# Seven block products instead of eight in the input product of a recurrent layer

## The chip, the cores and the metric

The kernel runs on one core of a Trainium2 chip. The metric is the device time of one execution in microseconds; of several runs the median is given. The core has five engines that run side by side, each with its own queue of instructions that it works off in order: TensorE (PE: matmuls; the loading of its weights is shown as PEld), VectorE (DVE), ScalarE (ACT), GpSimd (POOL) and SyncE (SP, which here only issues transfers). Matmuls read SBUF and add into banks of PSUM; DVE and ACT read both, POOL reads SBUF alone. Engines wait for each other by semaphores.

## The reference

One step of a streaming encoder with two layers over 640 tokens: 512 of a prompt and 8 sample sequences of 16. The first layer is recurrent (an RG-LRU), the second is attention over a shared K and V. What matters here is the first layer, cut from the reference:

```python
hn = rms_norm(x, g_pre[l]) * (1.0 + scale) + shift
...
xb, zg = jnp.split(hn @ w_in, 2, axis=-1)          # (640, 2048) @ (2048, 8192)
xb, conv_new = causal_conv(xb, conv0, conv_w, conv_b)
y, hT = rg_lru(xb, h0, w_r, b_r, w_i, b_i, lam)    # two block-diagonal gate products inside
return (y * jax.nn.silu(zg)) @ w_out, hT, conv_new
```

`hn @ w_in` is the input product: all 640 tokens against 8192 columns, of which the first 4096 are the branch that goes through the convolution and the recurrence (the x branch) and the others the gate branch.

## The kernel before

Everything is float32 in and out. Each operand of a large product is split into a high and a low part in the type fp32r, and a product takes three matmuls (`mm3`, lines 90 to 94): high times high, high times low, low times high. For weights, `wsplit` (line 66) loads a raw tile by SP, ACT copies it to the high part `wh` (line 78), and DVE subtracts to get the low part `wl` (line 79).

The program has stages. In the **start** the squares of x give the norm, the adaLN weights of 33.5 MB stream in (`ada_first`, eight buffers) and give scale and shift for 128 features at a time (a K step; there are 16), and each finished step of the normed input is multiplied at once with five column tiles of 128 columns (`fill`). In the **recurrent part** 16 blocks of 256 features follow (`recurrent_block`, line 436). A block j has:

- two column tiles of the x branch, 2j and 2j+1: `proj_unit` runs 16 K tiles, two halves of 320 tokens each, three matmuls each, in two banks `psu` and `psv`; then ACT evicts to `hb`, ACT and DVE do the convolution (`ca`, `xf`), and the result is split (`xh`, `xl`);
- two column tiles of the gate branch: the same products, and the sigmoid times the value on ACT and DVE (`zs`);
- 48 matmuls of the two gates (`psg2`), ACT's sigmoids, and for each of the two halves of 128 features the RG-LRU: a tanh and a square root on ACT, on DVE a reciprocal of 640 columns, several products, the scan, and the product with `zs`; POOL keeps the states and issues the store to DRAM (`yd`).

The weights of the recurrent part come from the generator `plan` in the order of their use; `ahead` (line 428) keeps up to three pairs of split tiles (`WB`) of 1024 columns ready, four raw tiles behind them. After the recurrent part comes the output product (`out_product`), then K and V, then attention; these stages are not touched, except for the pools of SBUF that they use.

The Tile framework puts the instructions of each engine in an order of its own by their place in the program and its idea of their durations, and adds the semaphores. At run time each engine keeps that order.

## Time and profile before

| | |
|---|---|
| time, median of 3 runs | 2955.97 us (2954.01 to 2956.94) |
| profiled execution, span | 2950.4 us; its own time is not listed apart from the three |
| TensorE busy in the span | 2904.2 us, 98% |
| recurrent part, first matmul of `psu` to first of the output product | 145.65 to 1089.01 us |
| matmuls in it | 59 column tiles x 96, and 768 of the gates |
| granted TensorE clock in it | 1.00 |

A row of groups in the profile names the line, the engine, the operation, what it writes and reads, and how often; then total busy time and mean nanoseconds of one, then idle time ahead of them and what ended it. A row of stretches gives for a stretch the busy time of each engine with its count of instructions, then the granted clock, the DMA share and GB/s. A row of the timeline has its start, its duration, the engine, the line and the operation; neighbours of one kind are merged ("x3").

### The profile page before, as it was taken

To read this page: it belongs to the slowest core of one execution; us is meant where nothing else is said; L and a number is where in the kernel's file an instruction comes from. 1 tells how busy PE (TensorE), PEld (TensorE's weight loads), DVE (VectorE), ACT (ScalarE), POOL (GpSimd) and SP (SyncE) were. 2 spreads that over 40 slices of the span, in tenths; PEclk is the share of its full clock that TensorE was granted. 3 is DMA by queue.
4 is the path that set the end of the run, shared out by engine and by line. 5 is a ranking of instruction groups with operands and counts; after the bars stand their busy time and mean duration, and the time that the engine had idled before them with its cause. 6 is when DMAs were issued, how large, how long until landed. Compare 5 with 4: busy or idle time off the path is not lost.

```text
span 2950.4 us, 48268 instructions
## 1 busy us (share of the span) xinstructions
PE 2904.2 (98%) x19414; PEld 2604.3 (88%) x19414; DVE 1890.5 (64%) x2491; ACT 1460.6 (50%) x2227; POOL 297.1 (10%) x518
## 2 busy tenths in 40 slices
PE   6999999999999999999999999999999999999998
PEld 5899999999999997778877999877989998897787
DVE  5686655666655666734468877777667666677435
ACT  3364434444434455634357666674455555556323
POOL 0010000000000000001021422000100000001000
PEclk9999999999999999999999999999999999999999
DMA  9822222222222237645477666663655556555736
GB/s 346 293 100 86 86 83 85 82 95 86 82 87 82 82 121 232 195 123 183 139 263 241 214 212 215 207 218 95 199 172 180 177 177 199 177 182 182 221 103 226
DMA packets 224512, 481.43 MB, mean 163 GB/s; under 512 B 17416, under 2 KB 106632, under 8 KB 223136
## 3 DMA queue, kind: packets, MB, share of 16 engines
q1 hardware_dynamic: 215216, 441.99, 46.8%
q0 software_dynamic: 9072, 36.37, 3.5%
q8 instruction: 152, 2.49, 0.3%
q14 instruction: 72, 0.59, 0.1%
HBM read 441.17 MB, written 37.11 MB: 162 GB/s over the span
## 4 chain that ended last, share of the span: by engine, by line
PE 94%; DVE 2%; DMA 2%; ACT 1%; issue 1%; POOL 0%; SPq 0%; DVEq 0%; POOLq 0%; ACTq 0%
PE acc L92 7%; PE acc L93 7%; PE acc L94 7%; PE psh L92 5%; PE acck L92 5%; PE psh L94 5%; PE psh L93 5%; PE acck L93 5%; PE acck L94 5%; PE psu L92 5%; PE psv L92 5%; PE psv L93 5%; PE psu L93 5%; PE psu L94 5%; PE psv L94 5%; PE psa L187 2%
## 5 line engine op out<-in xcount | busy, mean ns | idle before, releaser
L79 DVE TENSOR_TENSOR wl<-wr,wh 128x1024 fp32r<-128x1024 f32 (+2 forms) x382 | 448.9, 1176 | 443.2 <-ACT wh L78 441.7
L78 ACT ACTIVATE wh<-wr 128x1024 fp32r<-128x1024 f32 (+2 forms) x382 | 383.0, 1009 | 572.1 <-PE acc L94 219.1
L93 PE MATMUL acc<-wl,yh 128*128 128x512 f32 x960 | 376.3, 393 | 5.5 <-DVE wl L79 5.3
L92 PE MATMUL acc<-wh,yh 128*128 128x512 f32 x960 | 376.9, 393 | 4.3 <-ACT wh L78 2.1
L94 PE MATMUL acc<-wh,yl 128*128 128x512 f32 x960 | 375.2, 392 | 0.3 <-DVE yl L547 0.3
L175 DVE TENSOR_TENSOR wa<-wa,wa 128x1024 f32<-128x1024 f32 (+1 forms) x256 | 310.0, 1246 | 25.7 <-ACT wa L174 23.7
L92 PE MATMUL psh<-nh,wh 128*128 128x320 f32 x1024 | 323.9, 316 | 0.0
L94 PE MATMUL psh<-nh,wl 128*128 128x320 f32 x1024 | 318.9, 311 | 0.0
L93 PE MATMUL psh<-nl,wh 128*128 128x320 f32 x1024 | 317.4, 310 | 0.0
L174 ACT ACTIVATE wa<-wa 128x1024 bf16<-128x1024 f32 x256 | 262.9, 1052 | 67.9 <-DVE wa L175 49.0
L92 PE MATMUL psu<-hh,wh 128*128 128x320 f32 x944 | 291.7, 309 | 0.0
L92 PE MATMUL psv<-hh,wh 128*128 128x320 f32 x944 | 291.7, 309 | 0.0
L93 PE MATMUL psv<-hl,wh 128*128 128x320 f32 x944 | 291.7, 309 | 0.0
L94 PE MATMUL psv<-hh,wl 128*128 128x320 f32 x944 | 291.7, 309 | 0.0
L94 PE MATMUL psu<-hh,wl 128*128 128x320 f32 x944 | 291.7, 309 | 0.0
L93 PE MATMUL psu<-hl,wh 128*128 128x320 f32 x944 | 291.7, 309 | 0.0
L92 PEld LDWEIGHTS acc<-wh,yh 128*128 128x128 f32 x960 | 180.8, 189 | 52.9 <-issue 8.7
L93 PEld LDWEIGHTS acc<-wl,yh 128*128 128x128 f32 x960 | 181.1, 189 | 45.2 <-DVE wl L79 8.5
L94 PEld LDWEIGHTS acc<-wh,yl 128*128 128x128 f32 x960 | 181.3, 189 | 38.7 <-DVE yl L547 1.3
L92 PEld LDWEIGHTS psh<-nh,wh 128*128 128x128 f32 x1024 | 192.3, 188 | 19.3 <-DVE ql L881 12.6
L94 PEld LDWEIGHTS psh<-nh,wl 128*128 128x128 f32 x1024 | 192.4, 188 | 0.5 <-DVE wl L79 0.2
L93 PEld LDWEIGHTS psh<-nl,wh 128*128 128x128 f32 x1024 | 192.4, 188 | 0.1
(275 smaller groups left out, 6093.1 us busy)
## 6 DMA issues: line engine op xcount, KB each, us to landing
wa<-w_ada_dram SPq DMA_DIRECT2D x192, 512.0 KB, 4.8
wr<-w_in_a_dram SPq DMA_DIRECT2D x118, 512.0 KB, 3.7
wr<-w_out_a_dram SPq DMA_DIRECT2D x96, 512.0 KB, 4.1
wr<-w_in_b_dram SPq DMA_DIRECT2D x64, 512.0 KB, 5.1
ck<-cache_k_dram SPq DMA_DIRECT2D x64, 512.0 KB, 6.5
cv<-cache_v_dram SPq DMA_DIRECT2D x64, 512.0 KB, 5.4
wr<-w_out_b_dram SPq DMA_DIRECT2D x56, 512.0 KB, 4.0
wr<-w_v_dram SPq DMA_DIRECT2D x40, 512.0 KB, 4.2
```

Of the source, the lines that this page charges most:

```text
L78: nc.scalar.activation(hi[:, :n], raw[:, :n], AF.Copy)
L79: nc.vector.tensor_tensor(lo[:, :n], raw[:, :n], hi[:, :n].bitcast(F32), ALU.subtract)
L92: mm(out, sh, mh, start=start, stop=False, **kw)
L93: mm(out, sh, ml, start=False, stop=False, **kw)
L94: mm(out, sl, mh, start=False, stop=stop, **kw)
L174: nc.scalar.activation(parts[i], raw, AF.Copy)
L175: nc.vector.tensor_tensor(parts[2] if i else raw, raw, parts[i], ALU.subtract)
L187: nc.tensor.matmul(ps[32 * j : 32 * j + 32, :], self.c3[:, 4 * g + j, :], ws[j // 2][i][:, j % 2, :], start=g + i == 0, stop=g == 3 and i ...
```

## The change

Twelve of the 16 K tiles of the input product are taken as six pairs, (0, 1), (2, 3) and so on. For a pair of K tiles, a pair of column tiles and the two halves of the tokens, the product is one of 2x2 by 2x2 blocks. It is now computed by seven block products instead of eight, in Winograd's form of Strassen's scheme, and the four other K tiles (`PLAIN`) as they were.

- In the start `combine` makes four sums of blocks of the normed input for each pair of K tiles (`S1` to `S4`), on POOL, and splits them on ACT and DVE. They stay in SBUF for all 30 pairs of column tiles. The start multiplies four column tiles instead of five, and w_ada has five buffers instead of eight.
- `pair_weights` yields nine split tiles for a pair of column tiles: seven of 768 columns (b11, and sums of blocks) and two of 512 for the plain K tiles. The four sums are made by POOL in place in the raw tiles: the second set is b12 - b11 in the tile of b11, the third b22 minus that in the same tile, the sixth b22 - b12 in the tile of b12, the seventh b21 minus the third in the tile of b11.
- `pair_product` runs the sets in this order with accumulators in four banks: X11 into a, S1 into c, S2 into a again, X12 and the plain K tiles into b, S3 into a again, X22 and plain into d, S4 and plain into c, plain into a. Between two uses of a bank ACT copies what it holds (`keep`); the last evictions are DVE additions of a bank and such a copy.
- Three products with 640 columns a half block go from DVE to POOL: with the gate branch's sigmoid, of the input gate with x, and of the result with the gate branch.
- `ahead` keeps four pairs of split tiles (768 columns) with seven raw tiles. The states are stored and the parameters loaded block by block. The pools of the later stages are opened after the recurrent part, over the memory that it used, with waits by tile.

The core of the diff:

```diff
+NP = 6
+PLAIN = range(2 * NP, KD)
+WQ = NP * P
+WV = len(PLAIN) * P
+X12, X22, X11, S1, S2, S3, S4 = range(7)
+EARLY = (0, 1, FT, FT + 1)
...
-            ws = self.adap.tile([P, 4, 256], F32, tag="wa", name="wa0", bufs=8)
+            ws = self.adap.tile([P, 4, 256], F32, tag="wa", name="wa0", bufs=5)
...
+    def combine(self, rp, slot, even, odd):
+        nc, G = self.nc, self.nc.gpsimd
+        a, b = slice(0, HALF), slice(HALF, T)
+        t = [rp.tile([P, HALF], F32, tag=f"s{i}", name=f"s{i}", bufs=1) for i in range(4)]
+        G.tensor_tensor(t[0], even[:, b], odd[:, b], ALU.add)
+        G.tensor_tensor(t[1], t[0], even[:, a], ALU.subtract)
+        G.tensor_tensor(t[2], even[:, a], even[:, b], ALU.subtract)
+        G.tensor_tensor(t[3], odd[:, a], t[1], ALU.subtract)
+        for i, v in zip((S2, S3, S4, S1), (t[1], t[2], t[3], t[0])):
+            c = slice(HALF * i, HALF * i + HALF)
+            nc.scalar.activation(slot[:, 0, c], v, AF.Copy)
+            nc.vector.tensor_tensor(slot[:, 1, c], v, slot[:, 0, c].bitcast(F32), ALU.subtract)
...
+    def pair_weights(self, q):
+        w, G = self.I["w_in_a"][q], self.nc.gpsimd
+        at = iter(range(0, 4 * WQ, WQ))
+        b11, b12, b22, b21 = (self.wload(w[:, o : o + WQ]) for o in at)
+        yield self.hilo(b11, P)
+        G.tensor_tensor(b11, b12, b11, ALU.subtract)
+        yield self.hilo(b11, P)
+        G.tensor_tensor(b11, b22, b11, ALU.subtract)
+        yield self.hilo(b11, P)
+        yield self.hilo(b21, P)
+        G.tensor_tensor(b12, b22, b12, ALU.subtract)
+        v = self.wload(w[:, 4 * WQ : 4 * WQ + WV])
+        yield self.hilo(v, P)
+        yield self.hilo(b12, P)
+        G.tensor_tensor(b11, b21, b11, ALU.subtract)
+        yield self.hilo(b11, P)
+        v = self.wload(w[:, 4 * WQ + WV :])
+        yield self.hilo(b22, P)
+        yield self.hilo(v, P)
...
+        def seven(ps, i, first):
+            hi, lo = self.weights()
+            c = slice(HALF * i, HALF * i + HALF)
+            for n, x in enumerate(self.pairs):
+                self.mm3(ps, hi[:, n, :], lo[:, n, :], x[:, 0, c], x[:, 1, c], first and n == 0, n == NP - 1, **kw)
+            self.ahead()
...
+        a, c = bank("pa7"), bank("pc7")
+        seven(a, X11, True)
+        p1 = keep(a)
+        seven(c, S1, True)
+        p5 = keep(c)
+        seven(a, S2, False)
+        u2 = keep(a)
+        b = bank("pb7")
+        seven(b, X12, True)
+        w = self.weights()
+        plain(b, w, 0)
+        evac(0, 0, b, p1)
+        d = bank("pd7")
+        plain_d = lambda: plain(d, w, 1)
+        seven(a, S3, False)
+        u3 = keep(a)
+        seven(d, X22, True)
+        plain_d()
+        self.ahead()
+        evac(0, 1, d, u3)
+        seven(c, S4, False)
+        w = self.weights()
+        plain(c, w, 0)
+        evac(1, 0, c, u2)
+        plain(a, w, 1)
+        self.ahead()
+        evac(1, 1, a, p5)
...
+            G.tensor_tensor(zs[h], zs[h], g, ALU.mult)
...
-            V.tensor_tensor(ig, ig, xf[h], ALU.mult)
+            G.tensor_tensor(ig, ig, xf[h], ALU.mult)
...
-            V.tensor_tensor(hh, hh, zs[h], ALU.mult)
-            nc.gpsimd.dma_start(self.yd[P * f : P * f + P, :], hh)
+            G.tensor_tensor(hh, hh, zs[h], ALU.mult)
+            G.dma_start(self.yd[P * f : P * f + P, :], hh)
+        G.dma_start(self.O["state"][:, 2 * j : 2 * j + 2, :], st)
...
+            self.WB, self.RB, self.WW = 4, 7, WQ
```

Where the instructions of a middle block stand on their engines shows in three places. The first is POOL around the end of a block's second RG-LRU half. Before (`g` is the state sequence, `st` the kept states, `hb` the convolution's input):

```order
L520 COPY st<-g_5743 128x1
L521 COPY st<-g_5743 128x8
L523 DMA yd<-g_5743 128x640
L448 MEMSET hb 128x3
L449 COPY hb<-pv 128x8x3
L456 COPY st<-hb 128x3
L457 COPY st<-hb 128x24
```

And now:

```order
L664 COPY st<-g_4861 128x8
L665 TENSOR_TENSOR g_4861<-g_4861,zs 128x640
L667 DMA out_state_dram<-st 128x72
L666 DMA yd<-g_4861 128x640
L451 TENSOR_TENSOR wr<-wr 128x768
L583 COPY st<-hb 128x3
L584 COPY st<-hb 128x24
L456 TENSOR_TENSOR wr<-wr 128x768
L453 TENSOR_TENSOR wr<-wr 128x768
L460 TENSOR_TENSOR wr<-wr 128x768
```

The four weight sums (lines 451 to 460) of the next pair, that of the gate branch, stand behind the product and the two stores of the RG-LRU half, and the sum for the sixth set (456) ahead of that for the third (453).

The second is ACT from there on, where the convolution's start (`ca`), the split of its result (`xh`) and the weights' high parts (`wh`) meet. Before:

```order
L461 ACTIVATE ca<-hb,pv 128x664
L78 ACTIVATE wh<-wr 128x1024
L470 ACTIVATE xh<-xf 128x640
L452 ACTIVATE hb<-psu 128x320
L78 ACTIVATE wh<-wr 128x1024
L452 ACTIVATE hb<-psv 128x192
L454 ACTIVATE hb<-psv 128x8x16
L461 ACTIVATE ca<-hb,pv 128x664
```

And now:

```order
L588 ACTIVATE ca<-hb,pv 128x664
L86 ACTIVATE wh<-wr 128x768 x3
L597 ACTIVATE xh<-xf 128x640
L588 ACTIVATE ca<-hb,pv 128x664
L86 ACTIVATE wh<-wr 128x512
L498 ACTIVATE keep<-pa_6491 128x320
L86 ACTIVATE wh<-wr 128x768
L498 ACTIVATE keep<-pc_6492 128x320
```

The evictions are gone from ACT, and the copy of bank a after the first block product (`keep<-pa`) stands behind five splits and convolution steps of the block.

The third is DVE at the same place: from the scan of the second half (line 519 before, 662 now) on. Before:

```order
L519 SCALAR_TENSOR_TENSOR g_3335<-q,g_3335 128x640
L464 SCALAR_TENSOR_TENSOR xf<-hb,pv,ca 128x512
L522 TENSOR_TENSOR g_3335<-g_3335,zs 128x640
L466 SCALAR_TENSOR_TENSOR xf<-hb,pv,ca 128x128
L79 TENSOR_TENSOR wl<-wr,wh 128x1024
L471 TENSOR_TENSOR xl<-xf,xh 128x640
```

And now:

```order
L662 SCALAR_TENSOR_TENSOR g_5505<-q,g_5505 128x640
L87 TENSOR_TENSOR wl<-wr,wh 128x768
L568 TENSOR_TENSOR hb<-pd_5690,keep 128x192
L568 TENSOR_TENSOR hb<-pd_5690,keep 128x8x16
L590 SCALAR_TENSOR_TENSOR ca<-hb,pv,ca 128x664
L87 TENSOR_TENSOR wl<-wr,wh 128x768
L590 SCALAR_TENSOR_TENSOR ca<-hb,pv,ca 128x664
L591 SCALAR_TENSOR_TENSOR xf<-hb,pv,ca 128x512
L568 TENSOR_TENSOR hb<-pc_5575,keep 128x320
L87 TENSOR_TENSOR wl<-wr,wh 128x768
L568 TENSOR_TENSOR hb<-pa_5574,keep 128x192
L568 TENSOR_TENSOR hb<-pa_5574,keep 128x8x16
```

Three low parts of 768 columns stand between the convolution steps where one of 1024 stood, and the evictions of the four accumulators are here now.

More of the change, by code (lines that the diff above doesn't have):

```diff
@@ L189, in ada @@
             yield
-        m = self.mp.tile([P, 512], F32, tag="mod", name="msb", bufs=2)
+        m = self.more.tile([P, 512], F32, tag="mod", name="msb", bufs=2)
         nc.scalar.activation(m, ps, AF.Copy)
@@ L301, in norm_rows @@
             else:
-                sq = self.mp.tile([P, T], F32, tag="mod", name="sq", bufs=2)
+                sq = rp.tile([P, T], F32, tag="row", name="sq", bufs=4)
                 nc.scalar.activation(sq, x, AF.Square)
@@ L314, in spread @@
         nc = self.nc
-        dg = self.mp.tile([P, T], F32, tag="mod", name="diag", bufs=2)
+        dg = rp.tile([P, T], F32, tag="row", name="diag", bufs=4)
         for t in range(TT):
@@ L402, in proj_part @@
                          **(dict(skip_group_check=True) if shared else {}))
-    def proj_unit(self, f, banks=None):
-        if f in self.begun:
-            return self.begun[f]
-        u, v = banks or (self.acc("psu"), self.acc("psv"))
-        unit = (f, [(u[:, :HALF], 0, HALF, False), (v[:, :HALF], HALF, T, False)])
-        for kc in range(2):
-            self.proj_part(unit, range(8 * kc, 8 * kc + 8), self.weights())
-        self.ahead()
-        return unit[1]
     def plan(self):
-        I = self.I
-        for kc in range(2):
-            yield I["w_in_a"][3, :, 8 * kc : 8 * kc + 8, :], P
+        yield from self.pair_weights(1)
@@ new lines, with conv_rows @@
+    HW = 3 + TP + NB * (TS + 3)
+    S0 = 3 + TP
+    def conv_rows(self, j, ep):
+        G = self.nc.gpsimd
+        pv = ep.tile([P, 2, 40], F32, tag="pv", name="pv", bufs=3)
+        self.nc.sync.dma_start(pv, self.I["lru"][:, 2 * j : 2 * j + 2, :])
+        rows = []
+        for h in range(2):
+            hb = ep.tile([P, self.HW + 1], F32, tag="hb", name="hb", bufs=2)
+            G.memset(hb[:, 0:3], 0.0)
+            G.tensor_copy(hb[:, self.S0 : self.HW].rearrange("p (b t) -> p b t", t=TS + 3)[:, :, 0:3], pv[:, h, 8:32].rearrange("p (b t) -> p b t", t=3))
+            rows.append(hb)
+        return pv, rows
@@ L1109, in heads @@
         return out
-    WB = 3
+    ABUFS = {"A": NP, "V": KD - 2 * NP}
     AB = (3, 4)
```

287 lines of the change are left out of this document (174 added, 113 removed).

## The prediction

> **What bounds the kernel now.** I read the busy shares and the chain of waits first, then the stretches of the first layer's recurrent part, then the groups of DVE, ACT and POOL in it.
>
> ```profile
> span 2950.4 us, 48268 instructions
> PE 2904.2 (98%) x19414; PEld 2604.3 (88%) x19414; DVE 1890.5 (64%) x2491; ACT 1460.6 (50%) x2227; POOL 297.1 (10%) x518
> ...
> PE 94%; DVE 2%; DMA 2%; ACT 1%; issue 1%; POOL 0%; SPq 0%; DVEq 0%; POOLq 0%; ACTq 0%
> ...
> 145.65:208.90 63.25, 63.25 (x434) 63.25 (x433) 54.88 (x72) 40.76 (x63) 6.55 (x19) 1.00 0.26 88
> 208.90:1060.00 851.10, 851.10 (x5805) 851.10 (x5805) 526.72 (x623) 367.43 (x536) 69.94 (x192) 1.00 0.26 87
> ```
>
> TensorE is the bound. In the stretch that the change rewrites (the last two rows; columns PE, PEld, DVE, ACT, POOL, granted clock, DMA share, GB/s) it has no gap at all, at full clock, and its pace is 851.10/5805 = 0.1466 us a matmul. The 0.31 us of a single record overlaps with its neighbours, so matmuls are priced by the pace. DVE has 62% there, POOL 8%. The span lies 5.6 us under the median of 2955.97; I make the sum in the span and add that.
>
> **What it saves on TensorE.** A pair of 128-column tiles cost 2 x 16 x 2 x 3 = 192 matmuls of 320 columns. Now the twelve paired K tiles cost 7 x 6 x 3 = 126 and the four plain ones 48, so 174. Thirty pairs lie outside the start; column tile 2, which was in the start, comes back (96). A middle block (two pairs and 48 gate matmuls) goes from 432 to 396 matmuls, at the pace from 63.3 to 58.1 us; there are 14 of them. The two blocks ahead go from 384 to 444, from 56.3 to 65.1. If TensorE stays full, this sums to 14 x -5.28 + 8.8 = -65 us. That is the most the change can bring, and it asks the other engines for more in less time.
>
> **What it adds.** The splits of the weights go from 10 a block (eight of 1024, two of 512 columns) to 20 (fourteen of 768, six of 512), since seven sums of blocks have more elements than four blocks. And where a tile of weights lasted 48 matmuls (7 us) with three tiles ahead, one now lasts 18 (2.6 us) with four ahead: the lead falls from some 20 us to 8 to 10. The loads are not what comes late: a pair still brings 2.1 MB, DMA is at 26% there, and seven raw tiles let the next pair's loads start during the pair ahead.
>
> ```profile
> L79 DVE TENSOR_TENSOR wl<-wr,wh 128x768 fp32r<-128x768 f32 x8 | 7.6, 949 | 1.1 <-ACT wh L78 1.1
> ...
> L507 DVE RECIPROCAL q<-q 128x640 f32<-128x640 f32 x28 | 116.2, 4150 | 0.5
> L463 DVE SCALAR_TENSOR_TENSOR ca<-hb,pv,ca 128x664 f32<-128x664 f32 x52 | 47.2, 907 | 3.1 <-ACT ca L461 2.4
> L519 DVE TENSOR_TENSOR_SCAN g<-q,g 128x640 f32<-128x640 f32 x27 | 40.2, 1488 | 0.5
> L511 DVE TENSOR_TENSOR g<-g,g 128x640 f32<-128x640 f32 x27 | 22.4, 829 | 0.4
> L79 DVE TENSOR_TENSOR wl<-wr,wh 128x512 fp32r<-128x512 f32 x26 | 18.0, 693 | 77.3 <-ACT wh L78 76.9
> L506 DVE TENSOR_SCALAR q<-g 128x640 f32<-128x640 f32 x27 | 13.3, 494 | 9.1 <-ACT g L504 7.6
> L482 DVE TENSOR_TENSOR zs<-zs,psu 128x320 f32<-128x320 f32 x26 | 12.7, 488 | 139.9 <-ACT zs L481 139.9
> ...
> L466 DVE SCALAR_TENSOR_TENSOR xf<-hb,pv,ca 128x128 f32<-128x128 f32 x26 | 9.0, 347 | 0.0
> ```
>
> POOL gets eight weight sums of 768 columns and six products of 640 a block, where it had only short copies. Their prices come from its two-operand work elsewhere: 0.51 us for 128 columns and 1.30 for 512, so 2.06 ns a column, 1.83 us for 768 and 1.57 for 640.
>
> ```profile
> 2109.40 0.51 POOL L924 TENSOR_TENSOR e<-e,mask 128x128 f32<-128x128 f32 x1 [0.36 <-ACT e L908]
> 1363.93 1.30 POOL L646 TENSOR_TENSOR oacc<-oacc,gm 128x512 f32<-128x512 f32 x1 [72.86 <-ACT jk L590]
> L523 POOL DMA_DIRECT2D yd<-g x32 | 17.7, 552 | 36.0 <-DVE g L522 19.8 <-DVE xf L466 16.2
> L521 POOL COPY st<-g 128x8 f32<-128x8 f32 x32 | 6.1, 191 | 0.0
> ```
>
> A block asks 8 x 1.83 + 6 x 1.57 = 24 us of POOL. That would be no matter if POOL and DVE ran side by side, but the trace says that they do not:
>
> ```profile
> 1615.31 10.06 POOL L735 TENSOR_TENSOR wr<-wr,vec 128x1024 f32<-128x1024 f32 x4 [11.16 <-issue]
> 1618.46 7.99 DVE L738 TENSOR_TENSOR wl<-wr,wh 128x1024 fp32r<-128x1024 f32 x3 [0.59 <-ACT wh L737]
> ...
> 1640.39 4.76 DVE L175 TENSOR_TENSOR wa<-wa,wa 128x1024 f32<-128x1024 f32 x4
> ...
> 1362.40 2.05 DVE L644 TENSOR_TENSOR oacc<-acc,oacc 128x512 f32<-128x512 f32 x3 [0.23 <-PE acc L94]
> ```
>
> While POOL worked, three DVE splits took 7.99 us, 2.66 each; with POOL idle four subtractions of that size took 4.76, 1.19 each. They take turns, one whole instruction each. The last row has one operand in PSUM; it ran beside the POOL product at 1363.93 without growing (0.68 each). So DVE work on two SBUF tensors adds to POOL's and does not overlap it.
>
> **The loop that sets a block.** With the matmuls cheaper and the lead short, what decides is whether weights come in time. I follow one block from the end E of the gate-branch products, every step behind the one that it waits for or that stands ahead of it in its engine's order. In a full queue neighbours overlap by 0.05 us (four of 1.22 in 4.76), which I take off.
>
> ```profile
> L78 ACT ACTIVATE wh<-wr 128x768 fp32r<-128x768 f32 x8 | 6.7, 836 | 0.7 <-DMA wr<-w_in_a_dram 0.7
> ...
> L498 ACT ACTIVATE g<-psg,pv 128x320 f32<-128x320 f32 x108 | 51.7, 528 | 1.1
> L508 ACT ACT_TABLE_LOAD x28 | 35.9, 1283 | 0.5
> L461 ACT ACTIVATE ca<-hb,pv 128x664 f32<-128x664 f32 x26 | 24.5, 944 | 2.3
> L504 ACT ACTIVATE g<-g,k 128x640 f32<-128x640 f32 x27 | 22.6, 837 | 0.4
> L470 ACT ACTIVATE xh<-xf 128x640 fp32r<-128x640 f32 x26 | 19.3, 741 | 54.7 <-DVE xf L466 54.7
> L78 ACT ACTIVATE wh<-wr 128x512 fp32r<-128x512 f32 x26 | 16.3, 628 | 78.6 <-PE psv L93 78.6
> L452 ACT ACTIVATE hb<-psu 128x320 f32<-128x320 f32 x27 | 11.9, 439 | 99.8 <-PE psu L94 99.8
> ```
>
> 1. ACT: one split (0.84), the gate branch's sigmoid (as the tanh, 0.84), two gate sigmoids (1.06), tanh (0.84): E+3.6.
> 2. DVE from the first half's TENSOR_SCALAR to the second half's scan: two RG-LRU halves of 8.64 (reciprocal 4.15, scan 1.49, two products 1.64, two TENSOR_SCALAR 0.98, small ones 0.38), five splits of 768, two of 512, one eviction: 23.9, less 25 overlaps, 22.7: E+26.3.
> 3. POOL takes its turns in that stretch: a product, a sum and two copies fall outside the reciprocals, which I let run beside POOL: 3.6: E+29.9.
> 4. Behind the scan: DVE's next split (0.95), then POOL's two copies, the product with the gate branch, and two DMA issues, 3.0, all ahead of the next pair's first weight sum in POOL's order: E+33.9.
> 5. First sum 1.83; ACT's high part 0.84; POOL is by then in the sum for the sixth product, which holds DVE's low part back to E+37.9; low part 0.95; one convolution step 0.91 that DVE has next; third sum 1.83: E+41.6. Each sum works in place on the tile that the split before it reads, so they can't run ahead of each other.
> 6. ACT's high part of the third set 0.84, DVE's low part 0.95, then the two evictions of the last accumulator (0.33 each, 320 columns being 0.49) and the convolution's last step (0.35), which ACT needs for its split of x (0.74), the second half's convolution start (0.94), a split (0.63), and only then its copy of the first product (0.44): E+47.1, less a dozen overlaps, E+46.5.
> 7. That copy is what the third product waits for, since it adds into the same bank. From there 138 matmuls remain to the next E: 20.2 us.
>
> So a block takes 66.7 us, 8.6 over its matmuls' 58.1 and 3.4 over the 63.3 of before. TensorE waits in two places. Ahead of the x branch's product with the sixth set ACT's copy of the bank stands behind a table load (1.28) and a square root that need the second half's TENSOR_SCALAR at about E+18; it comes near E+21, and TensorE asks at E+19.5 (132 matmuls). That wait lies beside the loop and adds nothing to it. The other, 5 to 6 us, is step 7's. The bounds: without step 3's turns and with DVE served first in step 5, 61.8; without any wait 58.1; with the reciprocals' two POOL products and one sum added as well, 71.7. I take the middle, because the rows above show strict turns between the two engines.
>
> **The start and the rest.** In the start a K step takes 7.04 us, with DMA full until it ends:
>
> ```profile
> 24.01 3.64 PE L212 MATMUL pss<-wa,cT 128*32 128x256 f32 x32
> ...
> 113.15 1.93 PE L212 MATMUL pss<-wa,cT 128*32 128x256 f32 x32
> 120.19 1.93 PE L212 MATMUL pss<-wa,cT 128*32 128x256 f32 x32
> ...
> 126.00:132.00 6.00, 6.00 (x61) 4.77 (x60) 2.06 (x8) 1.62 (x3) 0.00 (x0) 1.00 0.91 352
> 132.00:140.00 8.00, 8.00 (x75) 6.77 (x74) 5.41 (x14) 3.11 (x6) 0.00 (x0) 1.00 0.22 68
> ```
>
> One column tile fewer is 1.05 MB, 3 us at 350 GB/s, and 6 matmuls less a step; the bound there is DMA. TensorE takes the first w_ada at 24.01 us; x and five buffers are 7.9 MB, 22.5 us of transfer, so five instead of eight lose little there. The four x sums on POOL a pair and their splits fit in 14 us. So -3 us, with bounds of -14 (TensorE alone) and +10 (a tenth lost to the fewer buffers). The first sets of weights ride behind w_ada and are hidden by the last K step's products. At the end the new pools lie where the old ones were; the 48 gate matmuls of the last block, 7 us, hide the first w_out_a loads: 0, at most +4.
>
> **Sum.** 14 x 3.4 = 47.6; the two blocks ahead 8.8 and half a block's wait 4.3, 13.1; the start -3. That is +57.7 on 2955.97: 3014 us.
>
> **The rivals.** *TensorE stays full.* All sums hide and -65 - 3 remains: 2888 us. For it speaks that DVE had 38% free; against it, that a block's DVE work on SBUF alone (splits 17.4, RG-LRU without reciprocals 9.0, convolution some 7, less overlaps, 31 us) and POOL's 24 with its copies, 26, fill 57 of 58 us if they take turns. 0.11. *DVE goes first at the port,* so that POOL falls into the reciprocals: the block of 61.8, 14 x -1.5 + 13.1 - 3 = -11, 2945 us. 0.20. *The clock falls as well.* After a wait the granted clock was halved for 3.4 us:
>
> ```profile
> 1308.60:1311.10 2.50, 0.43 (x2) 0.01 (x1) 0.84 (x2) 1.68 (x2) 0.00 (x0) 1.00 0.07 28
> 1311.50:1314.90 3.40, 3.02 (x8) 2.05 (x7) 0.94 (x2) 0.74 (x1) 0.00 (x0) 0.50 0.66 181
> 1315.00:1318.40 3.40, 3.40 (x16) 2.80 (x15) 0.60 (x1) 0.51 (x1) 0.00 (x0) 1.00 0.46 153
> ```
>
> Eight matmuls ran where sixteen would have. A wait of 5 to 6 us a block could cost 1.7 more each time, +24: 3038 us. (The Trainium skill, TensorE: Matmul & The Clock Gate, "Why this matters for your kernels", warns of gaps over about 3 us; in these rows little more than 2 us idle was enough. By the page this wait would cost as much.) I leave it out of the sum since part of the slow time would lie in the wait itself. 0.20. *The reciprocals hold the port too*: 71.7 a block, +70 more, 3084 us; the nearest row, the DVE work with one SBUF operand above, speaks against it. 0.07. (The Trainium skill, SBUF — State Buffer, "Who interferes with whom", says that a DVE instruction with at most one SBUF input, outside the two-port modes, does not contend. No run here shows a reciprocal beside POOL work; by that rule this rival falls away and the sum stays.) The forecast itself has 0.42.
>
> **How the numbers follow.** A change of under 0.2% (6 us) can't be told from none. Faster comes from the first rival and most of the second (0.29); 0.06 falls within 0.2%; slower has 0.65. The range leaves out the full gain below and the held reciprocals above: 2930 to 3045.
>
> **What would show it.** Right: in the middle blocks TensorE is busy for some 58 of about 66 us; the waits ahead of the third product name ACT's copies or splits; POOL sums last over 1.9 us where DVE is busy; DVE splits next to them reach 2 us or more. Wrong: PE without gaps there and POOL sums hidden (then 2888), or gaps in the first K steps (then the start's price is off), or a block well under 63 us.

## The result, and the profile after

The changed kernel takes 3108.07 us (median of four runs, 3105.59 to 3110.88) where the kernel before takes 2956.35 (four runs): a ratio of 1.0515, 95% interval 1.050 to 1.053. The direction was forecast, the size was not: 152 us slower instead of 58. The profiled execution has a span of 3106.0 us, 155.6 over that of before.

The head of the page and its chain of waits, kernel after:

```profile
span 3106.0 us, 48299 instructions
PE 2882.5 (93%) x18874; PEld 2561.3 (82%) x18874; DVE 2111.3 (68%) x2673; ACT 1574.8 (51%) x2406; POOL 755.1 (24%) x773
...
PE 58%; issue 15%; DVE 11%; POOL 7%; DMA 4%; ACT 4%; SPq 0%; POOLq 0%; DVEq 0%; ACTq 0%
```

TensorE has 540 matmuls fewer, but its share of the chain fell from 94% to 58%. DVE, POOL, ACT and the issue of instructions took its place. Four marks in the timeline (first gate matmul of blocks 1, 2 and 15, first matmul of the output product) divide the loss. The terms of the forecast stand beside it:

| stretch | before, us | after, us | longer by | forecast |
|---|---|---|---|---|
| span's start to the gates of block 1 | 194.9 | 213.1 | 18.2 | 10.1 |
| block 1 to 2 | 63.4 | 82.0 | 18.6 | 3.4 |
| blocks 2 to 15, 13 blocks | 823.7 (63.4 each) | 915.6 (70.4 each) | 91.9 | 44.2 |
| gates of block 15 to output product | 7.0 | 26.6 | 19.6 | 0 |
| output product to the span's end | 1861.4 | 1868.7 | 7.3 | 0 |

The waits of TensorE from 280 to 1200 us, then stretches (columns PE, PEld, DVE, ACT, POOL, clock, DMA share, GB/s): one block, then the wait ahead of a third product of the gate branch and what follows it.

```profile
PE pa L106 <- ACT keep L498: 118.1, 39, 6.3
```

```profile
435.70:506.40 70.70, 61.53 (x398) 60.48 (x398) 52.65 (x58) 33.54 (x50) 33.52 (x30) 0.95 0.25 78
407.50:414.00 6.50, 0.30 (x3) 0.03 (x1) 6.49 (x9) 3.98 (x7) 3.81 (x6) 0.73 0.05 10
414.00:417.30 3.30, 3.25 (x12) 3.25 (x13) 3.27 (x6) 1.75 (x3) 0.58 (x2) 0.51 0.53 178
417.30:420.60 3.30, 3.30 (x25) 3.30 (x24) 1.86 (x3) 1.22 (x3) 0.21 (x1) 1.00 0.37 120
```

All the waits named are for ACT's copy of a bank, three in each block: one of 6.3 us ahead of the gate branch's third product, and in the x branch one of 1.6 ahead of the third product and one of 1.2 ahead of the fifth, that with the sixth set. After the long one 12 matmuls run in the time of 25. The timeline shows what the copy stood behind:

```profile
400.38 1.87 POOL L451 TENSOR_TENSOR wr<-wr 128x768 f32<-128x768 f32 x1
...
405.21 2.45 POOL L453 TENSOR_TENSOR wr<-wr 128x768 f32<-128x768 f32 x1 [0.91 <-DVE wl L87]
405.99 2.23 DVE L591 SCALAR_TENSOR_TENSOR xf<-hb,pv,ca 128x512 f32<-128x512 f32 x1
409.61 1.80 POOL L460 TENSOR_TENSOR wr<-wr 128x768 f32<-128x768 f32 x1 [1.95 <-DVE wl L87]
409.92 1.64 DVE L593 SCALAR_TENSOR_TENSOR xf<-hb,pv,ca 128x128 f32<-128x128 f32 x1
...
411.59 0.74 ACT L597 ACTIVATE xh<-xf 128x640 fp32r<-128x640 f32 x1 [2.32 <-DVE xf L593]
412.23 0.92 ACT L588 ACTIVATE ca<-hb,pv 128x664 f32<-128x664 f32 x1
413.07 0.61 ACT L86 ACTIVATE wh<-wr 128x512 fp32r<-128x512 f32 x1
413.59 0.41 ACT L498 ACTIVATE keep<-pa 128x320 f32<-128x320 f32 x1
...
414.05 0.63 PE L106 MATMUL pa<-xs,wh 128*128 128x320 f32 x1 [6.25 <-ACT keep L498]
```

The product that is copied had ended at 404.8. The copy came 9 us later since ACT first split the convolution's result, which DVE made late. DVE's step of 512 columns took 2.23 us (0.75 with POOL idle) beside POOL's sum at 405.21, and its step of 128 columns 1.64 (0.35 before) beside the fourth sum, at 409.61.

At the end of the recurrent part:

```profile
1217.50:1237.20 19.70, 0.39 (x3) 0.12 (x1) 15.36 (x18) 7.21 (x11) 8.63 (x11) 0.63 0.28 93
1237.20:1243.20 6.00, 5.95 (x14) 4.41 (x15) 3.33 (x4) 1.75 (x2) 0.00 (x0) 0.50 0.59 198
```

```profile
1231.29 0.17 DVE L659 TENSOR_TENSOR g<-g,h0t 128x8 f32<-128x8 f32 x1
1231.42 0.07 DVE L660 MEMSET q<- 128x8 f32 x1
...
1231.54 0.34 SPq L101 DMA_DIRECT2D wr<-w_out_a_dram  x1
```

TensorE stood for 19.4 us and then ran six at half clock. The first load of w_out_a left 0.1 us after DVE's last use of `h0t`, a tile of 8 columns, had ended.

### The profile page after: what moved, and what is told of

It is laid out like the page before. It is cut to its first block, busy times and chain, and to the rows that moved or that the text cites. A ratio compares the mean times of both kernels' runs of the same rounds, so it can differ in the third digit from the quotient of the medians.

```text
span 3106.0 us, 48299 instructions
## 1 busy us (share of the span) xinstructions
PE 2882.5 (93%) x18874; PEld 2561.3 (82%) x18874; DVE 2111.3 (68%) x2673; ACT 1574.8 (51%) x2406; POOL 755.1 (24%) x773
## 4 chain that ended last, share of the span: by engine, by line
PE 58%; issue 15%; DVE 11%; POOL 7%; DMA 4%; ACT 4%; SPq 0%; POOLq 0%; DVEq 0%; ACTq 0%
PE acc L106 6%; PE acc L107 6%; PE acc L108 6%; PE psh L106 5%; PE acck L106 5%; PE psh L108 5%; PE psh L107 5%; PE acck L107 5%; PE acck L108 5%; DVE q L650 2%; DVE wl L87 2%; POOL g L665 2%; PE psa L202 2%; POOL wr L451 2%; DMA wa<-w_ada_dram 2%
## 5 line engine op out<-in xcount | busy, mean ns | idle before, releaser
L87 DVE TENSOR_TENSOR wl<-wr,wh 128x768 fp32r<-128x768 f32 (+2 forms) x534 | 581.1, 1088 | 500.0 <-ACT wh L86 496.5
L86 ACT ACTIVATE wh<-wr 128x768 fp32r<-128x768 f32 (+2 forms) x534 | 469.3, 885 | 759.8 <-PE acc L108 233.3
L190 DVE TENSOR_TENSOR wa<-wa,wa 128x1024 bf16<-128x1024 f32 (+1 forms) x256 | 306.6, 1233 | 24.4 <-ACT wa L189 22.2
L106 PE MATMUL pa<-xs,wh 128*128 128x320 f32 x540 | 185.6, 344 | 139.2 <-ACT keep L498 133.5
L106 PEld LDWEIGHTS pa<-xs,wh 128*128 128x128 f32 x540 | 112.8, 209 | 150.7 <-ACT keep L498 144.8
L106 PEld LDWEIGHTS psh<-nh,wh 128*128 128x128 f32 x1024 | 192.3, 188 | 19.3 <-DVE ql L1037 12.6
L107 PE MATMUL pa<-xs,wh 128*128 128x320 f32 x540 | 179.7, 333 | 0.0
L108 PE MATMUL pa<-xs,wl 128*128 128x320 f32 x540 | 179.3, 332 | 0.0
L106 PE MATMUL acck<-nh,wh 128*128 128x320 f32 x512 | 161.5, 315 | 0.0
L108 PE MATMUL acck<-nh,wl 128*128 128x320 f32 x512 | 158.2, 309 | 0.0
```

Of the source, the lines that this page charges most:

```text
L86: nc.scalar.activation(hi[:, :n], raw, AF.Copy)
L87: nc.vector.tensor_tensor(lo[:, :n], raw, hi[:, :n].bitcast(F32), ALU.subtract)
L106: mm(out, sh, mh, start=start, stop=False, **kw)
L107: mm(out, sh, ml, start=False, stop=False, **kw)
L108: mm(out, sl, mh, start=False, stop=stop, **kw)
L190: nc.vector.tensor_tensor(parts[2] if i else raw, raw, parts[i], ALU.subtract)
```

## The experiments

Times of one run each, unless an interval is given, beside medians of the kernel before of 2953 to 2956 us on the same chips. The runs of the kernel before spread over 7 us on one chip, so a few microseconds between two single runs say nothing. "A block" is the mean of blocks 2 to 14 by the gates' first matmuls.

### What the loop of a block hangs on

**early**: ACT's copy goes ahead of its split of the convolution's result.

```diff
@@ keep
-            nc.scalar.activation(t, ps, AF.Copy)
+            self.kept = nc.scalar.activation(t, ps, AF.Copy).ins
@@ pair_product, mid: the convolution, for the gate branch
         p1 = keep(a)
+        done = mid() if mid else None
@@ conv, first half, from block 2 on; the second half's ca likewise
-            A.activation(a, x, AF.Copy)
+            with self.tc.issue_after(self.kept) if kept and h == 0 else nullcontext():
+                A.activation(a, x, AF.Copy)
```

> In blocks 2 to 15 ACT's split of the convolution's result (and what follows it there) is put behind ACT's copy of the gate branch's first product; no work is added or left out. Theory of the loop: the third product waits for that copy alone, its weights have been ready 4.5 us earlier (409.5 against 414.05), so the gap falls from 6.6 to about 2 us, the clock does not fall behind it (1.5 us), and a block goes from 70.4 to 64.5 us: some 3025. Rival, weights: the sets come just in time one after the other, a wait for the fourth to seventh set takes the place of the gap; a block over 68.5 us, over 3080. Rival, full engines: POOL and DVE in turns fill the block, none under 67 us.

3026.7 us, a block of 64.9, as the loop said. The waits of TensorE, 280 to 1130 us:

```profile
PE pa L107 <- ACT keep L499: 66.5, 38, 2.4
PE pc L109 <- DVE wl L88: 0.5, 3, 0.2
```

So 81 of the 152 us went with this edit. It moved more than the copy of 0.4 us: for that the convolution went to another place in the program, and in the traces the high part of a plain set also stands ahead of ACT's split now, and the low parts of that set and of the next one ahead of convolution steps on DVE. POOL's order is the same. How much each of them brought was not tried apart.

**late**: POOL's work for a block's second half goes behind the next pair's first two sums (`flush` holds what stood at the end of `lru`).

```diff
@@ pair_weights
-        G.tensor_tensor(b11, b22, b11, ALU.subtract)
+        self.summed = G.tensor_tensor(b11, b22, b11, ALU.subtract).ins
@@ flush, called at the head of the next block's convolution
+              with self.tc.issue_after(self.summed) if h == 1 and j < 15 else nullcontext():
...
+                G.tensor_tensor(hh, hh, zs[h], ALU.mult)
```

> POOL's copies of the states, the product with the gate branch and the two stores of a block's second half are put behind the next block's two sums for the second and third set; no work is added or left out. Theory of the loop: the first sum can start when its raw tile is split, at 467.2 instead of 470.1, so a block falls by some 2.9 us to 67.5, 3065-3070. Rival: the sums are not on the path, DVE's own order (scan, convolution, splits) sets it; a block within 1 us of 70.4, over 3095.

3101.6 us, a block of 69.9: the rival's numbers, though not its reason, that the sums are not on the path. The timeline of this run says why:

```profile
398.02 1.85 POOL L452 TENSOR_TENSOR wr<-wr 128x768 f32<-128x768 f32 x1 [8.94 <-DVE wl L88]
...
406.14 2.32 POOL L674 TENSOR_TENSOR g<-g,zs 128x640 f32<-128x640 f32 x1
...
408.93 2.58 DVE L596 SCALAR_TENSOR_TENSOR xf<-hb,pv,ca 128x128 f32<-128x128 f32 x1
...
409.54 1.81 POOL L461 TENSOR_TENSOR wr<-wr 128x768 f32<-128x768 f32 x1
```

The gates of this block start at 366.6 us, those of the same block in the kernel after at 366.1. So the first sum did start 2.8 us sooner (31.5 us after the gates instead of 34.3). But what was moved now stands between the third sum and the fourth: the product at 406.14, and behind it the issue of the stores. So the fourth sum began 43.0 us after the gates instead of 43.5, and the convolution's step of 128 columns did not end before that sum did, 2.58 us instead of 1.64: it ended at +45.0 instead of +45.5. All but 0.5 of the 2.8 us were given back within 14 us, since POOL's work had only changed its place. (The framework's order of the convolution's steps on DVE changed a little in this run as well.)

**nosums** leaves the sums out, so what it computes is not the product.

```diff
@@ pair_weights
-        G.tensor_tensor(b11, b12, b11, ALU.subtract)
...
-        G.tensor_tensor(b11, b21, b11, ALU.subtract)
```

> The four weight sums of a pair are left out (the raw blocks are split and multiplied as they are, so the output is not the reference's); POOL keeps the three products and the stores. Theory of the loop: without the sums the splits run ahead, DVE does not wait at the port, and the copy comes at some 406 us where TensorE needs it at 407.2; a block of 58 to 60 us, 2925-2960. Rival: the in-order queues of ACT and DVE alone hold the copy back (it stands behind the convolution either way); a block over 64 us, over 3015.

2922.9 us, a block of 58.4, full clock:

```profile
325.90:384.30 58.40, 58.37 (x399) 58.10 (x398) 46.49 (x58) 33.54 (x50) 15.93 (x21) 1.00 0.31 94
```

The matmuls alone need 58.06. The twenty splits, the copies and POOL's products all fit beside them; what does not fit is the sums on POOL. ACT's copy still stands behind its split of the convolution's result in this run, and nothing waits for it: without the sums that place costs nothing. DVE's busy time in a block is 46.5 us without them and 52.6 with them, though DVE does the same work in both: some 6 us of it are waits for POOL's sums, spent inside DVE's instructions.

### The clock

**warm** fills the long wait with matmuls that no one needs.

```diff
@@ pair_product, warm in the gate branch alone
         p5 = keep(c)
+        b = bank("pb7")
+        if warm:
+            x = self.pairs[0]
+            for _ in range(36):
+                nc.tensor.matmul(b, x[:, 0, 0:P], x[:, 0, 0:HALF], start=True, stop=True, **kw)
         seven(a, S2, False)
```

> The changed kernel with 36 matmuls more in each gate branch from block 1 on, just ahead of its third product, into the bank that is still free; they need nothing that is late, and their result is overwritten. They fill 5.3 of the 6.6 us in which TensorE waits, so the work in the wait is nothing, and the clock should not fall. Theory: the fallen clock lies on the loop through the 138 matmuls that follow the copy, 1.5 us a block, so a block goes from 70.4 to 68.8-69.0 and the time from 3108 to 3085-3090. Rival: the slow matmuls only fill a wait that comes later (the next one, ahead of the x branch's sixth set, grows by as much); block and time stay within 0.3 and 5 us.

3068.8 us, a block of 68.4. The stretch around the filled wait, and a block:

```profile
426.40:494.80 68.40, 64.59 (x435) 63.37 (x434) 52.64 (x58) 33.45 (x50) 33.52 (x30) 1.00 0.26 81
407.00:420.00 13.00, 13.00 (x91) 13.00 (x90) 6.74 (x10) 4.24 (x7) 0.79 (x2) 1.00 0.48 143
```

From block 1 to block 15 the clock does not fall any more, and more work made the kernel 39 us faster; the orders on ACT, DVE and POOL in a block are those of the kernel after. So the fallen clock cost 2.0 us a block, and block 1 came down by 7.6 as well: more than the 1.5 expected, and not hidden in a later wait. Some 6 of the 39 us are not the edit's: they lie behind the first matmul of the output product, where the clock happened to fall at two places instead of four.

### POOL or DVE for the sums and products

Three runs start from **early**. **earlysums** takes the sums to DVE, **earlyprods** the products, and **earlylatebound** keeps all on POOL but adds late and bound (below).

```diff
@@ pair_weights (earlysums)
-        w, G = self.I["w_in_a"][q], self.nc.gpsimd
+        w, G = self.I["w_in_a"][q], self.nc.vector
@@ silu_gates (earlyprods; the same for ig and hh in lru)
-            G.tensor_tensor(zs[h], zs[h], g, ALU.mult)
+            nc.vector.tensor_tensor(zs[h], zs[h], g, ALU.mult)
```

> On top of the run with ACT's copy ahead of the split (3026.7, a block of 64.7): the eight weight sums of a block go from POOL to DVE, at 0.95 instead of 1.85 us each, and POOL keeps the three products and the stores. Theory, turns: DVE no longer waits for sums on POOL and the sum of the second set does not stand behind the stores, so the third set is ready some 5 us earlier and its wait goes; a block of 59.5-61, 2950-2975. Rival, full DVE: its own work is then some 55 us of a block of 58 and no order fits it; a block of 63 or more, over 3005.

> On top of the run with ACT's copy ahead of the split (3026.7, a block of 64.7): the three products of 640 columns go back from POOL to DVE, so POOL keeps the sums, the copies of the states and the stores. Theory, turns: six POOL products of 1.57 us take turns with DVE, on DVE they cost 0.83 each, and the sum for the second set no longer stands behind a product; the third set is ready some 2.5 us earlier, a block of 61-62 and 2970-2990. Rival, full DVE: five microseconds more on DVE between the gates and the scan make the next sums later; a block of 65 or more, over 3030.

> Three edits together: ACT's copy ahead of the split of the convolution's result, POOL's second store behind the next two sums, and the two small tiles out of the way of the later weights pool. Theory: with the copy out of the way the weights of the third set are the last to come, and the later store brings its sum 2.9 us forward: a block from 64.7 to 62.3 us (a wait of 2 us ahead of the x branch's sixth set stays), and 10 us less at the end: 2980-2990. Rival: as in the run with the store alone, turns with the moved product take back what the sum gains; a block over 64, 3010-3020.

| run | us | a block | forecast of the theory |
|---|---|---|---|
| early | 3026.7 | 64.9 | 64.5 |
| earlysums | 2955.8 | 60.3 | 59.5 to 61 |
| earlyprods | 3015.1 | 63.7 | 61 to 62 |
| earlylatebound | 3013.7 | 64.9 | 62.3 |

The sums are the edit that counts. A block of earlysums, and its groups on DVE from 300 to 900 us:

```profile
395.50:455.80 60.30, 58.58 (x397) 58.06 (x397) 53.53 (x67) 33.36 (x50) 20.52 (x21) 1.00 0.29 92
```

```profile
L454 DVE TENSOR_TENSOR wr<-wr 128x768 f32<-128x768 f32 x20 | 19.1, 956 | 0.3
...
L596 DVE SCALAR_TENSOR_TENSOR xf<-hb,pv,ca 128x512 f32<-128x512 f32 x20 | 14.9, 744 | 0.4
...
L598 DVE SCALAR_TENSOR_TENSOR xf<-hb,pv,ca 128x128 f32<-128x128 f32 x20 | 6.9, 344 | 0.0
```

A sum takes 0.95 us on DVE, and the steps of the convolution are back at their durations of before. DVE is busy for 53.5 us, 0.9 more than with the sums on POOL: the waits of some 6 us were nearly as long as the sums themselves, eight of 0.95. The products back on DVE were worth 1.2 us a block, less than thought; the result lies between the two expectations. In earlylatebound the later store gave nothing, again; the wait moved on to DVE's low part of the next set (up to 2.1 us).

**sumsdve** has the sums on DVE as its only edit (the line above).

> The changed kernel with one edit: the eight weight sums of a block go from POOL to DVE; ACT's copy stays behind the split of the convolution's result. Theory, turns: the loop stays the same, but its sums take 0.95 instead of 1.85 us, convolution steps and small DVE operations no longer wait for a sum on POOL, and the sum of the second set does not stand behind POOL's stores; the copy comes some 43.5 instead of 48 us after the gates' start, so a block goes from 70.4 to 63.5-64.5 and the time to 3010-3025. Rival: the place of the copy in ACT's order is nearly all of it, and DVE with 7.6 us more gives back what the turns cost; a block of 68 or more, over 3070.

2955.4 us, a block of 60.3: neither number, and that of earlysums. The expectation had a wrong premise, that the copy would stay where it was. The framework sets the order by its own idea of durations, and without POOL's sums it put the copy first, as the timeline of this run shows:

```profile
492.86 0.41 ACT L498 ACTIVATE keep<-pa 128x320 f32<-128x320 f32 x1
495.12 0.74 ACT L597 ACTIVATE xh<-xf 128x640 fp32r<-128x640 f32 x1 [1.84 <-DVE xf L593]
```

So sumsdve shows that the sums on POOL, with all that hangs on them, make the kernel after 153 us slower than it is with them on DVE, but alone it could not say how much is the copy and how much the turns. **reorder** leaves the sums on POOL and takes the copy off the path in another way: between two uses of the first bank another bank's products run.

```diff
@@ pair_product
         seven(c, S1, True)
         p5 = keep(c)
-        seven(a, S2, False)
...
         seven(b, X12, True)
...
+        seven(a, S2, False)
         u2 = keep(a)
...
-        seven(a, S3, False)
-        u3 = keep(a)
         seven(d, X22, True)
...
+        seven(a, S3, False)
+        u3 = keep(a)
@@ pair_weights yields the sets in the same order
```

> The changed kernel (sums on POOL) with the nine products of a pair in another order: X11, S1, X12 with plain, S2, X22 with plain, S3, S4, so that between two uses of the first bank another bank's products run, and the weights of the third set need no sum. No work is added or left out. Theory, copy: the wait was ACT's copy between two uses of one bank; it now has 4.4 us more, and the sum for S2 as well, so 6.6 us of wait falls to about 2 and the clock does not fall behind it; a block of 63-65 us, 3005-3030. Rival, turns: DVE and POOL in turns set the pace of the weights and the copy is only where it shows; a block over 67, over 3060.

3048.7 us, a block of 67.2. The waits of TensorE, 400 to 900 us:

```profile
PE pd L108 <- DVE wl L87: 30.9, 15, 3.9
PE pb L108 <- DVE wl L87: 4.4, 8, 0.6
PE pd L106 <- ACT wh L86: 4.0, 5, 0.8
```

No wait for a copy is left, and 3.2 of the 10 us between 70.4 and earlysums' 60.3 are gone; the rest stands as waits for parts of weights, nearly all for low parts. The block is the one that the turns gave, the time lies between the two theories. But the new order also puts the set of X22, the first in bank d, straight behind the one that it is made from, and the longest wait, 3.9 us, is for that set: so reorder does not price the turns apart. What the runs show together is that the copy is where the delay shows first, and that with the copy out of the way weights come too late while POOL makes the sums (here, and in earlylatebound). Only the sums on DVE, or none, ended both.

### The end of the recurrent part

**bound** moves two tiles.

```diff
-            with self.pool("lru") as lp, self.pool("w7") as self.wp, self.pool("A") as self.ap:
+            with self.pool("lru", side="right") as lp, self.pool("w7") as self.wp, self.pool("A") as self.ap:
```

> Two small tiles of the recurrent part (the state h0t and the constants k4) move to the other end of SBUF, so that the later weights pool does not lie over them; nothing else changes. Theory: the first load of w_out_a waited only for the last DVE instruction on h0t, so it can go when the last raw tiles are split, some 25 us earlier; TensorE's gap of 19.7 us between the last gate product and the output product falls under 3 us, and the time from 3108 to 3081-3088. Rival: the output product waits for the last blocks' y anyway, or for another late tile under the new pools; then the gap stays over 12 us and the time over 3100. The blocks stay at 70.4 us either way.

3098.3 us. From the gates of block 15 to the output product it is now 12.6 us instead of 26.6, so the theory of the tile holds for 14 us; the gap itself falls from 19.4 to 5.4 us, between the two expectations. The time fell by only 10 us, since the stretches ahead came out 3.4 us longer in this run and the one behind 1.2. What is left of the gap is a wait that neither theory had, in the timelines of ACT and TensorE:

```profile
1224.96 1.05 ACT L86 ACTIVATE wh<-wr 128x1024 fp32r<-128x1024 f32 x1
...
1226.69 0.80 PE L106 MATMUL acc<-wh,yh 128*128 128x512 f32 x1 [5.38 <-ACT yh L702]
1229.25 0.79 PE L107 MATMUL acc<-wl,yh 128*128 128x512 f32 x1 [1.76 <-DVE wl L87]
```

The first load of w_out_a left at 1204.99 us and had landed at 1208.5, but ACT split it only at 1224.96: the splits of w_out_a and y stand in ACT's and DVE's orders between the steps of the last RG-LRU.

### Towards a version that beats both

**best4** puts together early, the sums on DVE, bound, a second buffer for the input gate, and parameters and k4 earlier; **best5** adds an order at the end; **best6** has the order of reorder and no forced order on ACT.

```diff
@@ lru (best4, best5, best6)
-                v = ep.tile([P, T], F32, tag=f"g{i}", name=f"g{i}", bufs=2 - i)
+                v = ep.tile([P, T], F32, tag=f"g{i}", name=f"g{i}", bufs=2)
@@ out_product (best5), behind the first loads and splits of y
+                    self.tc.add_manual_dep(self.behind[0], self.yl.name, info, reason="order")
+                    self.tc.add_manual_dep(self.sg, self.hi.name, info, reason="order")
```

> On top of the run with the early copy and the sums on DVE (2955.8, a block of 60.3): the two small tiles out of the way of the later weights pool, a second buffer for the input gate (so that ACT's last sigmoids no longer wait for DVE, with the copy behind them), the first two blocks' parameters loaded ahead of the weights, and the constants k4 computed in the middle of the start. Theory: the one wait left in a block, 1.4 us, goes: 58.3-58.7 a block; 13 us less at the end and 3 at the start: 2905-2918. Rival: the wait only moves to ACT's copy of the third product behind the square root; a block of 59.8 or more, 2930-2940.

> As the run before it, and the last block's reciprocal and sigmoid are queued behind the first split of w_out_a and of y, so that the output product does not wait for the last RG-LRU. Theory: the rest of the gap between gates and output product (8 us) goes, with the fallen clock behind it: 8 to 12 us less than the run before, 2895-2908, 1.6 to 2% faster than the kernel before. Rival: its second and third weights and the stores of the last y wait just as long and the gap comes back a little later; within 4 us of the run before.

> The new order of the products, with the sums on DVE, the two small tiles out of the way of the later pool, the second buffer of the input gate, and the parameters and constants ahead, but without an order forced on ACT or on the last block. Theory, copy: the two waits of 0.5 to 0.6 us for copies and what clings to them go from the block of 60.2: 58.3-59 us, 2905-2922, 1.2 to 1.8% faster than the kernel before. Rival, full DVE: DVE has some 55 us of work in a block of 58, and the last 2 us are weights that come late; 59.8 or more, 2930-2940.

best4 takes 2935.4 us. best5 takes 2935.9 (median of four), 0.993 of the kernel before, 95% interval 0.9913 to 0.9947, so it beats both kernels, the one before by 0.7%. best6 takes 2976.5, a ratio of 1.0078 (1.0061 to 1.0095). In best4 and best5 the rival was right; best6 is slower than either of its expectations. In best5 a block stays at 60.2; its waits from 300 to 900 us:

```profile
PE pa L107 <- ACT keep L500: 9.2, 20, 0.6
PE pa L109 <- DVE wl L88: 4.6, 10, 0.5
```

The wait of 1.4 us became three of about half a microsecond. The forced order at the end gave nothing: the waits of TensorE for splits, 4.5 and 3.0 us, became 5.2 and 0.9, and ACT's first split of w_out_a still stands behind the gate sigmoids of the last RG-LRU. In best6 a block takes 63.1, with waits of up to 2.7 ahead of bank b, for the low part of X12's set: with the sums on DVE the copies cost little, and the late set costs more. Whether that comes from the new order or from ACT's free one was not tried apart.

## Why the prediction was right and wrong

**Right.** Slower; TensorE no longer the bound in the middle blocks; the loop and its place. Its steps, read off in the block whose gates start at 366.1 us:

| step | forecast | measured |
|---|---|---|
| 3. scan of the second half ends | +29.9 | +30.5 |
| 4. first sum begins | +33.9 | +34.3 |
| 5. third sum ends | +41.6 | +41.6 |
| 6. the copy ends | +46.5 | +47.9 |
| 7. next gates | +66.7 | +69.7 |

That step 5 agrees to the tenth is in part luck: the scan ends 0.6 late, and the stretch from step 4 to 5 takes 0.4 less. The wait ahead of the third product is 6.3 us (5 to 6 forecast), and the one of the x branch ahead of the sixth set 1.2 (1.5). That this wait adds nothing to the loop, as forecast, no run shows. The other wait there, 1.6 us ahead of the third set, was not forecast. That the reciprocals do not hold the port is shown in the kernel after:

```profile
440.92 2.09 POOL L453 TENSOR_TENSOR wr<-wr 128x768 f32<-128x768 f32 x1
441.35 4.15 DVE L650 RECIPROCAL q<-q 128x640 f32<-128x640 f32 x1
...
442.97 1.57 POOL L652 TENSOR_TENSOR g<-g,xf 128x640 f32<-128x640 f32 x1
...
448.40 1.61 POOL L652 TENSOR_TENSOR g<-g,xf 128x640 f32<-128x640 f32 x1 [3.85 <-ACT g L641]
448.53 1.51 DVE L658 TENSOR_TENSOR h0t<-q,pv 128x8 f32<-128x8 f32 x1
...
463.98 0.15 DVE L658 TENSOR_TENSOR h0t<-q,pv 128x8 f32<-128x8 f32 x1
```

A product of POOL runs inside the reciprocal at its own 1.57 us, and the reciprocal keeps its 4.15. The next product of POOL, at 448.40, makes a DVE product of 8 columns wait: 1.51 us instead of 0.15. (The Trainium skill, SBUF — State Buffer, "Who interferes with whom", draws the line there: two SBUF inputs contend, one outside the two-port modes does not. Both rows agree.)

**Wrong**, by 98 us of span: 48 in blocks 2 to 14, 15 in block 1, 8 ahead of it and 27 at the end. The terms that failed:

1. *The clock was left out of the sum* "since part of the slow time would lie in the wait itself". It does not: the matmuls behind the wait lie on the loop. The rival of the fallen clock priced it at 1.7 us a block; warm measured 2.0, 27 us over 13 blocks, and 7.6 in block 1. It should have stood in the sum.
2. *Step 6* took the convolution's last step at 0.35 us. Beside POOL's sum it took 1.64, until that sum had ended. In the block of the table this step came 1.4 us later than forecast behind step 5, and step 7, with the clock down, 1.6 later behind step 6: together its 3.0 us. Over the 13 blocks the forecast was short by 3.7 each, 48 us.
3. *The first blocks.* One loop was worked out and applied to all. Block 1 is 18.6 us longer, not 3.4. There the gates wait 4.4 us, and the third product 9.5 instead of 6.3, with the clock down for 10 us in it and behind it. warm brought block 1 from 82.0 to 74.3 and earlysums to 65.6; what holds the rest was not tried. The start to block 1 is 18.2 longer, not 10.1. The last K step came 7.0 us sooner than before (127.28 instead of 134.27), not 3, but the first sets were not "hidden by the last K step's products": TensorE stood ahead of the first of the seven products, since ACT's evictions of the start's tiles stood behind splits that waited 4.1 us for a sum of POOL. Without the sums (nosums) this wait is 1.2 us, and the stretch 5.6 longer than before.

```profile
143.97 0.63 PE L106 MATMUL pa<-xs,wh 128*128 128x320 f32 x1 [5.76 <-ACT hb L563]
```

4. *"At the end the new pools lie where the old ones were; [...] 0, at most +4."* It cost 27 us: 19.6 up to the output product, and 7.3 after it, of which 3 are the six microseconds at half clock. The step asked whether the gate matmuls hide the first loads, and not which of the old tiles comes free last: the 8 columns of `h0t`. That the two tiles moved are worth 14 us is shown (bound); 5.4 more are the splits behind the last RG-LRU's work; where the last 4 us went is open.

The rival that TensorE stays full (2888) holds for the middle blocks once the sums are gone: nosums has 58.4 a block where it has 58.1. Its time is 2922.9, and the end is most of the difference.

## What to carry to other kernels

Work that is moved to POOL is not free because POOL is idle: where both engines read SBUF on two operands, count part of it on DVE as well (here eight sums of 1.85 us or more made DVE's instructions 6 us longer a block), and for a short DVE step of the loop allow for a whole POOL instruction. Find the loop from one use of a bank to the next and look for the short instruction in it that stands behind a long wait in its engine's order; here an edit that put a copy of 0.4 us first, and weight splits with it, brought 81 us. When pools are opened over old memory, look for the smallest and longest-lived tile under the first load.

## What the runs showed of the hardware that was not expected

- A DVE TENSOR_SCALAR with one SBUF input also waits for POOL, while the reciprocal, with one input too, does not. The kernel after has one beside a product of POOL, 1.28 us, and one with POOL idle, 0.48:

```profile
438.68 2.28 POOL L619 TENSOR_TENSOR zs<-zs,sg 128x640 f32<-128x640 f32 x1
440.03 1.28 DVE L649 TENSOR_SCALAR q<-g 128x640 f32<-128x640 f32 x1 [0.49 <-ACT g L647]
...
447.26 0.48 DVE L655 TENSOR_SCALAR q<-q 128x640 f32<-128x640 f32 x1
```

  (The Trainium skill, in the section named above, lists `tensor_scalar` among the operations that can enter a two-port mode, which fits.)
- Whether a wait halves the clock is decided by where it falls. In early the same wait of 2.38 us stands in each of the 13 blocks; the clock fell behind it in 4, and such a block is 1.4 to 1.5 us longer. Two of these waits, and the stretches behind them:

```profile
331.21 0.42 PE L107 MATMUL pa<-xs,wh 128*128 128x320 f32 x1 [2.38 <-ACT keep L499]
...
397.19 0.42 PE L107 MATMUL pa<-xs,wh 128*128 128x320 f32 x1 [2.38 <-ACT keep L499]
```

```profile
331.00:336.30 5.30, 5.09 (x24) 5.09 (x25) 5.26 (x7) 3.48 (x6) 3.17 (x5) 0.68 0.26 88
396.90:402.30 5.40, 5.11 (x35) 5.11 (x36) 5.36 (x7) 3.89 (x7) 3.27 (x5) 1.00 0.30 97
```

  All changes of the granted clock in a run lie on a grid of 3.41 us. The first of the two waits (328.83 to 331.21) lies whole between two lines of the grid, and the clock falls at the next line, 331.56; the second (394.82 to 397.19) is cut by a line at 396.41 into 1.59 and 0.79 us, and the clock stays. So it is in all 13 blocks: the four waits behind which the clock fell have 2.0 to 2.4 us between two lines, the other nine at most 1.9. A fifth fall comes behind another wait, of 2.0 us, in the x branch. In earlylatebound the waits of 2.1 us divide in the same way, 1.96 or more (9 fell) from 1.89 or less (4 did not). Waits of 1.4 us (earlysums) never halved the clock in 13 blocks, those of 6.3 always, for 6.8 or 10.2 us. (The Trainium skill, TensorE: Matmul & The Clock Gate, "What's actually happening", describes a free-running window of 3413 ns; the grid agrees. The Trainium skill, TensorE: Matmul & The Clock Gate, "Why this matters for your kernels", warns of gaps over about 3 us; here 2.4 was enough in 4 of 13 blocks, so the measurement decides.)
